# S5's V and W on one engine, attention's copies on another, K's rows on a queue of their own

## The chip, the cores and the metric

The kernel runs on one core of a Trainium2 chip. The metric is device time in microseconds for one launch. The engines' names in the profile are PE (TensorE, matmuls) and PEld (its weight loads), DVE (VectorE), ACT (ScalarE), POOL (GpSimd) and SP (SyncE); a "q" behind a name is the engine's instruction queue, which also issues transfers.

## The reference, cut to what matters

Two blocks of a diffusion transformer on 256 latent and 256 context tokens, width 1024, all in float32. Block 0 mixes tokens with grouped-query attention, block 1 with an S5 state space; each is followed by a hierarchical mixture of 32 experts.

```python
def gqa_axial_attention(u_lat, u_ctx, cos, sin, w_qkv, q_gain, k_gain, w_o, need_ctx):
    def project(u):
        q, k, v = split(u @ w_qkv)               # 8 heads of Q, 2 of K and V, 128 wide
        return rmsnorm(q, q_gain), rmsnorm(k, k_gain), v
    ...                                          # rope on the latent q and k only
    o = softmax(q k^T * hd ** -0.5) v            # context attends to context, latent to both
    y = o @ w_o

def s5_discretise(a_re, a_im, log_dt, b_re, b_im):   # 2 directions, 64 groups, 64 states, 16 channels
    dt = exp(log_dt)[:, None]
    ab = exp(a * dt)                             # complex
    bb = (ab - 1) / a * b
    ...
def s5_chunk_scan(u, ab, bb, c, s):
    x[t] = ab * x[t - 1] + bb @ u[t]
    y[t] = re(c @ x[t])

y = u * d_skip + scan(u) + flip(scan(flip(u)))   # then gelu, a linear unit with a gate, the residual
```

The S5 parameters do not depend on the tokens, so the operators that the scan needs are built while attention runs. The scan goes by blocks of 8 tokens: V holds B times the powers of the state's factor (tokens into state), W holds C times the powers (state into tokens), K is the kernel of one block (tokens into tokens), with the skip on its diagonal.

## The kernel before

**Attention** works on four tiles of 128 tokens, t = 0 and 1 the context, 2 and 3 the latent tokens. First each tile's K and V columns are projected (`project(t, 2)`), then twelve rounds of an outer loop follow, n = 0 to 11. In round n the loop runs side by side, one step of each at a time: `project(n % 4, n // 4)` for a half of Q (n < 8), `scores` for the half that was projected three rounds earlier, `values` for the one of four rounds earlier, and `steps(5, 2)`, which is five turns of two steps each of the background generator `par.work`. Between rounds stand a half of a modulation column (`mod.half`) and the transposes of Q (`turn_q`). Every engine executes its instructions in the order in which they were written, so this interleaving is the schedule.

`project` takes squares and a copy of the projection on ScalarE, their sum on VectorE (L359), the reciprocal root on GpSimd (`rstd`, L190, one power of 128 x 4 elements), then multiplies on VectorE: by the norm (L363), and by the gain (L365, context tiles) or by the rope tables (L371, L373, L374, latent tiles). `scores` has a matmul (L400), VectorE's maximum (L404), ScalarE's exponential (L405) and VectorE's reciprocal and scaling (L408, L409). `values` transposes the weights on TensorE, copies each transpose to SBUF (pT) and multiplies by V's half (L427). `evac` is a copy from PSUM, by turns on VectorE (L95) and ScalarE (L97).

**The background generator** `work` goes over 32 units of two S5 groups; four units share one set of operands (`operands`, L1245 to L1254, ten products on VectorE). A unit's `products` makes V in five VectorE operations (L1288, L1289, L1290, L1302, L1303) and W in five GpSimd operations of the same shape (L1297, L1298, L1299, L1304, L1305), each of 128 x 256 elements and with two inputs in SBUF. One unit later `turn` transposes V, copies it on ScalarE (vt, L1315) and sends it to DRAM by ScalarE's queue (L1317). Two units later `kernels` sends W by the same queue (L1323) and multiplies it on TensorE with `bd`, the block-diagonal operand (L1330). After four units `finish` copies the result on VectorE (ks, L1336, in a buffer of vt's), adds two pieces (L1340, L1341), sends four pieces of K's rows by ScalarE's queue (L1343, L1344), and copies the next operands into `bd` on VectorE (L1261, L1262). The generator has 145 steps; what the rounds leave over runs behind them (`bg.finish`).

Behind attention `tail` lends the SBUF of the stage to new buffers and SyncE's queue loads layer 1's modulation weights into them; the output projection (`out`, L443) follows, then the experts.

Of the kernel before, what the change touches and what calls it, by code (L numbers as in the profile page):

```python
# [9 lines left out]
F32 = mybir.dt.float32  # L10
# [4 lines left out]
AF = mybir.ActivationFunctionType  # L15
OP = mybir.AluOpType
# [227 lines left out]
def attention(c, mod, par, tail):  # L244
# [3 lines left out]
    with ExitStack() as ctx:  # L248
# [94 lines left out]
        def project(t, b):  # L343

            n = 2 if b == 2 else 4
            i = 1 if b == 2 else 0
            acc = bank("acc")
            for k in range(KT):
                if k and k % 2 == 0:
                    yield  # L350
                nc.tensor.matmul(acc, uT[:, k, 128 * t:128 * t + 128], wq[b][k // 4][:, k % 4, :],  # L351
                                 start=(k == 0), stop=(k == KT - 1))
            yield
            q = pk.tile([128, 4, HD], F32, name="qk", tag="qk", bufs=3)[:, 0:n]
            sq = pk.tile([128, 4, HD], F32, name="sq", tag="sq", bufs=2)[:, 0:n]
            nr = pk.tile([128, 4], F32, name="nr", tag="nr", bufs=2)[:, 0:n]
            nc.scalar.activation(sq.rearrange("p h d -> p (h d)"), acc[:, 0:128 * n], AF.Square)
            nc.scalar.activation(q.rearrange("p h d -> p (h d)"), acc[:, 0:128 * n], AF.Copy)
            nc.vector.tensor_reduce(nr, sq, axis=AX.X, op=OP.add)  # L359
            rstd(c, nr, nr, HD)  # L360
            if b == 2:
                nc.vector.tensor_copy(vv[:, t, :], acc[:, 256:512])
            nc.vector.tensor_mul(q, q, nr[:, :, None].to_broadcast([128, n, HD]))  # L363
            if t < 2:
                nc.vector.tensor_mul(q, q, gb[:, i:i + 1, :].to_broadcast([128, n, HD]))  # L365
            else:
                s5 = sq.rearrange("p h (a s f) -> p h a s f", a=2, s=2)
                q5 = q.rearrange("p h (a s f) -> p h a s f", a=2, s=2)
                sn = tab[:, t - 2, 1, i, :].rearrange("p (a s f) -> p a s f", a=2, s=2)
                for w in range(2):  # L370
                    nc.vector.tensor_mul(s5[:, :, :, w, :], q5[:, :, :, 1 - w, :],  # L371
                                         sn[:, None, :, w, :].to_broadcast([128, n, 2, 32]))
                nc.vector.tensor_mul(q, q, tab[:, t - 2, 0, i:i + 1, :].to_broadcast([128, n, HD]))  # L373
                nc.vector.tensor_add(q, q, sq)  # L374
            rot[t, b] = q
# [3 lines left out]
        def turn_k(t):  # L379
            p = bank("pt")  # L380
            for g in range(2):
                nc.tensor.transpose(p[:, 128 * g:128 * g + 128], rot[t, 2][:, g, :], c.ident)
            c.evac(kT[:, :, 128 * t:128 * t + 128], p[:, 0:256].rearrange("p (h d) -> p h d", h=2))

        def turn_q(t, g):
            x = lk.tile([128, 4, HD], F32, name="qT", tag="qT", bufs=3)
            p = bank("pt")
            for h in range(4):
                nc.tensor.transpose(p[:, 128 * h:128 * h + 128], rot[t, g][:, h, :], c.ident)
            c.evac(x, p.rearrange("p (h d) -> p h d", h=4))  # L390
            qT[t, g] = x

        P = {}
# [17 lines left out]
        def values(t, g):  # L411
            nk = 2 if t < 2 else 4
            yield
            pts = []
            for kt in range(nk + 1):
                if kt < nk:
                    p = bank("pt")
                    for h in range(4):
                        nc.tensor.transpose(p[:, 128 * h:128 * h + 128], P[t, g, h][:, 128 * kt:128 * kt + 128], c.ident)
                    x = lk.tile([128, 512], F32, name="pT", tag="pT", bufs=3)  # L420
                    c.evac(x, p)
                    pts.append(x)
                if kt == 1:
                    o = bank("acc")
                if kt:
                    k = kt - 1
                    nc.tensor.matmul(o, vv[:, k, 128 * g:128 * g + 128], pts[k], start=(k == 0), stop=(k == nk - 1))  # L427
                yield
            c.evac(oT[:, 4 * g:4 * g + 4, 128 * t:128 * t + 128], o.rearrange("p (h q) -> p h q", h=4))

        def rows():
            m2 = wk.tile([128, KT, 512], F32, name="m2", tag="uT").rearrange("p (j q) n -> p j (q n)", j=4)
# [20 lines left out]
                yield  # L453

        for t in range(4):
            together(project(t, 2), steps(5))
            if t:
                turn_k(t - 1)
        early.close()
# [3 lines left out]
            for h in range(2):  # L463
                fill[2 * ch + h - 3] = (ch, h)
        for n in range(12):
            s = [steps(5, 2)]
            if n < 8:
                s.append(project(n % 4, n // 4))
            if 0 <= n - 3 < 8:
                s.append(scores((n - 3) % 4, (n - 3) // 4))  # L470
            if 0 <= n - 4 < 8:
                s.append(values((n - 4) % 4, (n - 4) // 4))
            together(*s)
            if n == 0:
                turn_k(3)
            if n in fill:
                mod.half(0, *fill[n])
            if 0 <= n - 2 < 8:
                turn_q((n - 2) % 4, (n - 2) // 4)
            if n == 8:  # L480
                m2 = rows()
# [542 lines left out]
class S5Params:  # L1024
# [231 lines left out]

    def blocks(self, s):

        V = self.c.nc.vector
        for i in range(2):  # L1260
            V.tensor_copy(self.bd[i][0:64, :, 0:16], s[0:64, i])  # L1261
            V.tensor_copy(self.bd[i][64:128, :, 32:48], s[64:128, i])  # L1262

    def fetch(self, n):
        bc = self.wk.tile([128, 4, CH, 16], F32, name="bc", tag="bc", bufs=2)
# [3 lines left out]
    def work(self, bank, kbank):  # L1269
# [11 lines left out]
        def products(u, bc, s):  # L1281
            g, lg = slice(2 * u, 2 * u + 2), slice(2 * (u % per), 2 * (u % per) + 2)
            P = [x[:, g, ::-1][:, :, :, None].to_broadcast(sh) for x in self.P[1]]
            B = [s[:, i, lg][:, :, None, :].to_broadcast(sh) for i in (0, 2, 3)]
            vl = wk.tile([128, 2, 2, 128], F32, name="vl", tag="vl", bufs=2)
            v = [vl[:, i].rearrange("p g (i c) -> p g i c", i=8) for i in range(2)]
            v1 = wk.tile(sh, F32, name="v1", tag="v1")
            V.tensor_tensor(v1, B[0], P[2], op=OP.mult)  # L1288
            V.tensor_tensor(v[0], B[2], P[1], op=OP.mult)  # L1289
            V.tensor_tensor(v[1], B[1], P[0], op=OP.mult)  # L1290
            P = [x[:, g, :, None].to_broadcast(sh) for x in self.P[0]]
            C = [x[:, :, None, :].to_broadcast(sh) for x in (bc[:, 2, lg], s[:, 4, lg], s[:, 5, lg])]
            w = wk.tile([128, 2, 2, 128], F32, name="w", tag="w", bufs=5)
            wv = [w[:, :, i].rearrange("p g (i c) -> p g i c", i=8) for i in range(2)]
            w1 = wk.tile(sh, F32, name="w1", tag="w1")

            G.tensor_tensor(w1, C[0], P[2], op=OP.mult)  # L1297
            G.tensor_tensor(wv[0], C[2], P[1], op=OP.mult)  # L1298
            G.tensor_tensor(wv[1], C[1], P[0], op=OP.mult)  # L1299
            Q[u] = vl, w, s  # L1300
            yield
            V.tensor_tensor(v[0], v1, v[0], op=OP.subtract)  # L1302
            V.tensor_tensor(v[1], v1, v[1], op=OP.add)  # L1303
            G.tensor_tensor(wv[0], w1, wv[0], op=OP.subtract)  # L1304
            G.tensor_tensor(wv[1], wv[1], w1, op=OP.subtract)  # L1305
            yield

        def turn(u):
            vl, w, _ = Q[u]
            p = bank()  # L1310
            for i in range(2):
                for k in range(2):
                    nc.tensor.transpose(p[:, 256 * k + 128 * i:256 * k + 128 * i + 128], vl[:, i, k], c.ident)
            vt = wk.tile([128, 512], F32, name="vt", tag="vt", bufs=3)
            A.activation(vt, p, AF.Copy)  # L1315
            o = slice(512 * (u % per), 512 * (u % per) + 512)
            A.dma_start(self.vd[u // per][:, o], vt)  # L1317
# [13 lines left out]
                                     start=(i == 0), stop=(i == 1), skip_group_check=True)  # L1331

        def finish(n):
            ks = wk.tile([128, per, 128], F32, name="ks", tag="vt", bufs=3)
            kv = Q["kv"]
            V.tensor_copy(ks, kv)  # L1336
            gq = slice(per * n, per * n + per)
            for q in range(2):
                f, b = 64 * q, 64 * q + 32
                V.tensor_tensor(ks[f:f + 16, :, 0:16], kv[b:b + 16, :, 112:128], ks[f:f + 16, :, 0:16], op=OP.add)  # L1340
                V.tensor_add(ks[f:f + 16, :, 0:16], ks[f:f + 16, :, 0:16], self.dm[f:f + 16, gq])  # L1341
                dst = self.kd.rearrange("c (g q) n -> c q g n", q=2)[:, q, gq]
                A.dma_start(dst[:, :, 112:240], ks[f:f + 16])  # L1343
                A.dma_start(dst[:, :, 0:112], ks[b:b + 16, :, 0:112])  # L1344
            if n + 1 < NG // CH:
                self.blocks(Q[per * n + per][2])

# [509 lines left out]
```

## Time and profile before

| | |
|---|---|
| time, median of 3 runs | 1219.82 us (1219.55 to 1220.65) |
| profiled execution | 1219.71 us |
| its span, first to last instruction | 1217.9 us |
| busy in the span: PE, DVE, POOL, ACT | 1057.2, 802.1, 388.3, 270.0 us |
| mean granted TensorE clock | 0.948 of full speed |
| HBM traffic | 266 GB/s over the span |

A busy share is an average over stages with different limits; the change lies in the stage from about 45 to 314 us. A matmul that waits inside the pipeline counts as busy in places. An instruction's recorded time can overlap with the next one's on the same engine, so for a price both the recorded time and the distance from start to start are read.

### The profile page before, as it was taken

Reading aid. Unit: us, or ns where it says so; the run is one execution under the profiler, and the core shown is the slowest. Engines: PE = TensorE matmul, PEld = TensorE weight load, DVE = VectorE, ACT = ScalarE, POOL = GpSimd, SP = SyncE. Lnnn points to the kernel's source line nnn. Section 1 sums busy time; section 2 is a strip of 40 time slices with the busy share of each in tenths; the row PEclk is TensorE's granted clock in tenths of the full one; section 3 lists DMA queues with packets and bytes.
Section 4 is the critical chain, followed back from the end, with each engine's and each line's share of the span. In section 5 each row is a group of like instructions: output and inputs, shape, how many; then the busy total and the mean of one; then the engine's idle time right before and its main releaser. Section 6 shows DMA issues by size and latency. Waiting matters only on the chain. (4 is left out here: it accounts for less than half of the span.)

```text
span 1217.9 us, 18285 instructions
## 1 busy us (share of the span) xinstructions
PE 1057.2 (87%) x7011; PEld 619.4 (51%) x7011; DVE 802.1 (66%) x1679; ACT 270.0 (22%) x511; POOL 388.3 (32%) x473
## 2 busy tenths in 40 slices
PE   2888888857999799999999987787995999999997
PEld 0443444424444556666655543376674555555553
DVE  7788787888345526767778786588887344444444
ACT  3311223222112211111121211322433222112210
POOL 3566364554322202222355653346532000000000
PEclk9998899978999899999999999788997999999999
DMA  9845654652898488888676686669967799999951
GB/s 303 320 147 164 214 198 134 225 199 73 299 396 307 152 339 323 331 321 321 255 270 241 263 333 259 166 150 266 343 221 323 297 371 382 382 372 382 382 230 35
DMA packets 86892, 325.52 MB, mean 267 GB/s; under 512 B 9720, under 2 KB 19416, under 8 KB 68368
## 3 DMA queue, kind: packets, MB, share of 16 engines
q1 hardware_dynamic: 69296, 293.20, 65.9%
q10 hardware_dynamic: 13408, 20.01, 5.0%
q0 software_dynamic: 4096, 11.09, 2.8%
q8 instruction: 58, 0.95, 0.3%
q14 instruction: 34, 0.28, 0.1%
HBM read 305.37 MB, written 18.89 MB: 266 GB/s over the span
## 5 line engine op out<-in xcount | busy, mean ns | idle before, releaser
L801 PE MATMUL gu<-ring,xq 128*64 128x256 f32 x1136 | 162.1, 390 | 7.5 <-POOL pt L723 4.4
L870 POOL TENSOR_TENSOR h<-h,z 128x512 f32<-128x512 f32 x64 | 83.9, 1334 | 179.4 <-DVE z L857 179.4
L801 PE MATMUL gu<-more,xq 128*64 128x256 f32 x912 | 132.3, 387 | 1.7 <-DVE sl L806 1.7
L801 PEld LDWEIGHTS gu<-ring,xq 128*64 128x64 f32 x1136 | 91.6, 139 | 70.3 <-issue 30.8
L857 DVE TENSOR_TENSOR z<-co,gate 128x512 f32<-128x512 f32 x128 | 85.4, 685 | 40.7 <-PE co L866 31.3
L866 PE MATMUL co<-yh,oT 128*128 128x512 f32 x188 | 87.4, 465 | 16.8 <-DVE z L857 8.3
L801 PEld LDWEIGHTS gu<-more,xq 128*64 128x64 f32 x912 | 74.4, 138 | 50.6 <-issue 20.1
L351 PE MATMUL acc<-ring,uT 128*128 128x512 f32 x192 | 95.2, 629 | 4.7 <-ACT uT L327 3.4
L753 PEld LDWEIGHTS xt<-gq,parts 128*128 128x128 f32 x672 | 87.3, 191 | 10.5 <-issue 6.9
L753 PE MATMUL xt<-gq,parts 128*128 128x256 f32 x672 | 91.6, 286 | 0.0
L805 ACT ACTIVATE sl<-gu 64x256 f32<-64x256 f32 x64 | 24.1, 377 | 251.7 <-PE gu L801 251.7
L866 PE MATMUL co<-yl,oT 128*128 128x512 f32 x188 | 78.1, 415 | 0.6 <-DVE yl L851 0.6
L814 DVE COPY hT<-ht 128x128 f32<-128x128 f32 x64 | 18.4, 287 | 86.8 <-PE ht L812 86.6
L822 PE MATMUL y<-ring,hT 128*64 128x512 f32 x288 | 69.7, 604 | 0.4 <-DVE hT L814 0.4
L866 PEld LDWEIGHTS co<-yh,oT 128*128 128x128 f32 x188 | 35.8, 190 | 50.8 <-DVE z L857 19.9
L789 ACT ACTIVATE xq<-xt 128x512 f32<-128x512 f32 x56 | 33.4, 597 | 119.5 <-PE xt L753 119.5
L806 DVE TENSOR_TENSOR sl<-gu,sl 64x256 f32<-64x256 f32 x64 | 27.3, 426 | 47.0 <-ACT sl L805 45.7
L351 PEld LDWEIGHTS acc<-ring,uT 128*128 128x128 f32 x192 | 35.5, 200 | 40.2 <-issue 34.3
L822 PE MATMUL y<-more,hT 128*64 128x512 f32 x224 | 54.1, 604 | 0.4 <-DVE hT L814 0.4
L870 DVE TENSOR_TENSOR h<-h,z 128x512 f32<-128x512 f32 x64 | 50.5, 788 | 2.2
L141 PE MATMUL gv<-ring,cT 128*32 128x256 f32 x512 | 35.2, 420 | 18.3 <-DVE rs L189 16.3
L868 DVE TENSOR_TENSOR h<-h,co 128x512 f32<-128x512 f32 x64 | 41.1, 682 | 5.7 <-PE co L866 5.7
(424 smaller groups left out, 1954.8 us busy)
## 6 DMA issues: line engine op xcount, KB each, us to landing
ring<-moe_w_up SPq DMA_DIRECT2D x36, 1024.0 KB, 8.5
ring<-moe_w_down SPq DMA_DIRECT2D x36, 1024.0 KB, 9.4
ring<-moe_w_gate SPq DMA_DIRECT2D x35, 1024.0 KB, 6.8
ring<-mod_w SPq DMA_DIRECT2D x32, 1024.0 KB, 8.0
more<-moe_w_gate SPq DMA_DIRECT2D x29, 1024.0 KB, 7.0
more<-moe_w_up SPq DMA_DIRECT2D x28, 1024.0 KB, 9.2
more<-moe_w_down SPq DMA_DIRECT2D x28, 1024.0 KB, 11.2
more<-mod_w SPq DMA_DIRECT2D x16, 1024.0 KB, 8.7
```

The costliest lines, as they stand in the source:

```text
L141: nc.tensor.matmul(self.bank[i, b][32 * q:32 * q + 32, o:o + 256], self.cT[:, k, :], self.tiles[i, ch, k // 2][:, k % 2, 256 * q:256 * q + ...
L351: nc.tensor.matmul(acc, uT[:, k, 128 * t:128 * t + 128], wq[b][k // 4][:, k % 4, :], start=(k == 0), stop=(k == KT - 1))
L753: self.c.nc.tensor.matmul(p, x[:, k, :], g, start=(n + i == 0 and first), stop=(n + 1 == self.nt and i == 1), skip_group_check=True)
L789: nc.scalar.activation(out[-1][:, 2 * (s % 2):2 * (s % 2) + 2], p.rearrange("p (k n) -> p k n", k=2), AF.Copy)
L801: nc.tensor.matmul(p[s:s + 64, 0:HID], xT[k], w[k // 4][:, k % 4, :], start=(k == 0), stop=(k == KT - 1), skip_group_check=True)
L805: nc.scalar.activation(sl, p[0:64, 0:HID], AF.Silu)
L806: nc.vector.tensor_tensor(sl, p[64:128, 0:HID], sl, op=OP.mult)
L822: self.c.nc.tensor.matmul(p[o:o + 64, :], hT[:, f, :], wd[f][:, 512 * n:512 * n + 512], start=(f == 0), stop=(f == 1), skip_group_check=True)
L857: self.c.nc.vector.tensor_tensor(z, p, self.gate[j][:, 512 * f:512 * f + 512], op=OP.mult)
L866: nc.tensor.matmul(p, oh[:, 128 * n:128 * n + 128], y, start=(i == 0), stop=(i + 1 == len(rows)))
L868: nc.vector.tensor_tensor(h, h, p, op=OP.add)
L870: (nc.gpsimd if f else nc.vector).tensor_tensor(h, h, self.gated(p, j, f), op=OP.add)
```

## The change

V's and W's ten operations are all on VectorE, in four steps of the generator (V's three products, W's three, V's two sums, W's two) where there were two; the turns take two steps in the K and V part and three in the rounds. The copies of vv, kT, qT, pT and oT, which were VectorE's or alternated, are ScalarE's, and so are `bd`'s. On context tiles the two multiplications behind the norm become one fused operation for each head. K's rows have a buffer of their own (ks), vt has two in place of three, and the four transfers of a group are issued from GpSimd.

```diff
--- before.py
+++ after.py
@@ -359,11 +359,12 @@
             nc.vector.tensor_reduce(nr, sq, axis=AX.X, op=OP.add)
             rstd(c, nr, nr, HD)
             if b == 2:
-                nc.vector.tensor_copy(vv[:, t, :], acc[:, 256:512])
-            nc.vector.tensor_mul(q, q, nr[:, :, None].to_broadcast([128, n, HD]))
+                nc.scalar.activation(vv[:, t, :], acc[:, 256:512], AF.Copy)
             if t < 2:
-                nc.vector.tensor_mul(q, q, gb[:, i:i + 1, :].to_broadcast([128, n, HD]))
+                for h in range(n):
+                    nc.vector.scalar_tensor_tensor(q[:, h], q[:, h], nr[:, h:h + 1], gb[:, i, :], op0=OP.mult, op1=OP.mult)
             else:
+                nc.vector.tensor_mul(q, q, nr[:, :, None].to_broadcast([128, n, HD]))
                 s5 = sq.rearrange("p h (a s f) -> p h a s f", a=2, s=2)
                 q5 = q.rearrange("p h (a s f) -> p h a s f", a=2, s=2)
                 sn = tab[:, t - 2, 1, i, :].rearrange("p (a s f) -> p a s f", a=2, s=2)
@@ -380,14 +381,14 @@
             p = bank("pt")
             for g in range(2):
                 nc.tensor.transpose(p[:, 128 * g:128 * g + 128], rot[t, 2][:, g, :], c.ident)
-            c.evac(kT[:, :, 128 * t:128 * t + 128], p[:, 0:256].rearrange("p (h d) -> p h d", h=2))
+            nc.scalar.activation(kT[:, :, 128 * t:128 * t + 128], p[:, 0:256].rearrange("p (h d) -> p h d", h=2), AF.Copy)
 
         def turn_q(t, g):
             x = lk.tile([128, 4, HD], F32, name="qT", tag="qT", bufs=3)
             p = bank("pt")
             for h in range(4):
                 nc.tensor.transpose(p[:, 128 * h:128 * h + 128], rot[t, g][:, h, :], c.ident)
-            c.evac(x, p.rearrange("p (h d) -> p h d", h=4))
+            nc.scalar.activation(x, p.rearrange("p (h d) -> p h d", h=4), AF.Copy)
             qT[t, g] = x
 
         P = {}
@@ -418,7 +419,7 @@
                     for h in range(4):
                         nc.tensor.transpose(p[:, 128 * h:128 * h + 128], P[t, g, h][:, 128 * kt:128 * kt + 128], c.ident)
                     x = lk.tile([128, 512], F32, name="pT", tag="pT", bufs=3)
-                    c.evac(x, p)
+                    nc.scalar.activation(x, p, AF.Copy)
                     pts.append(x)
                 if kt == 1:
                     o = bank("acc")
@@ -426,7 +427,7 @@
                     k = kt - 1
                     nc.tensor.matmul(o, vv[:, k, 128 * g:128 * g + 128], pts[k], start=(k == 0), stop=(k == nk - 1))
                 yield
-            c.evac(oT[:, 4 * g:4 * g + 4, 128 * t:128 * t + 128], o.rearrange("p (h q) -> p h q", h=4))
+            nc.scalar.activation(oT[:, 4 * g:4 * g + 4, 128 * t:128 * t + 128], o.rearrange("p (h q) -> p h q", h=4), AF.Copy)
 
         def rows():
             m2 = wk.tile([128, KT, 512], F32, name="m2", tag="uT").rearrange("p (j q) n -> p j (q n)", j=4)
@@ -453,7 +454,7 @@
                 yield
 
         for t in range(4):
-            together(project(t, 2), steps(5))
+            together(project(t, 2), steps(5, 2))
             if t:
                 turn_k(t - 1)
         early.close()
@@ -463,7 +464,7 @@
             for h in range(2):
                 fill[2 * ch + h - 3] = (ch, h)
         for n in range(12):
-            s = [steps(5, 2)]
+            s = [steps(5, 3)]
             if n < 8:
                 s.append(project(n % 4, n // 4))
             if 0 <= n - 3 < 8:
@@ -1256,10 +1257,10 @@
 
     def blocks(self, s):
 
-        V = self.c.nc.vector
+        A = self.c.nc.scalar
         for i in range(2):
-            V.tensor_copy(self.bd[i][0:64, :, 0:16], s[0:64, i])
-            V.tensor_copy(self.bd[i][64:128, :, 32:48], s[64:128, i])
+            A.activation(self.bd[i][0:64, :, 0:16], s[0:64, i], AF.Copy)
+            A.activation(self.bd[i][64:128, :, 32:48], s[64:128, i], AF.Copy)
 
     def fetch(self, n):
         bc = self.wk.tile([128, 4, CH, 16], F32, name="bc", tag="bc", bufs=2)
@@ -1288,21 +1289,23 @@
             V.tensor_tensor(v1, B[0], P[2], op=OP.mult)
             V.tensor_tensor(v[0], B[2], P[1], op=OP.mult)
             V.tensor_tensor(v[1], B[1], P[0], op=OP.mult)
+            yield
             P = [x[:, g, :, None].to_broadcast(sh) for x in self.P[0]]
             C = [x[:, :, None, :].to_broadcast(sh) for x in (bc[:, 2, lg], s[:, 4, lg], s[:, 5, lg])]
             w = wk.tile([128, 2, 2, 128], F32, name="w", tag="w", bufs=5)
             wv = [w[:, :, i].rearrange("p g (i c) -> p g i c", i=8) for i in range(2)]
             w1 = wk.tile(sh, F32, name="w1", tag="w1")
 
-            G.tensor_tensor(w1, C[0], P[2], op=OP.mult)
-            G.tensor_tensor(wv[0], C[2], P[1], op=OP.mult)
-            G.tensor_tensor(wv[1], C[1], P[0], op=OP.mult)
+            V.tensor_tensor(w1, C[0], P[2], op=OP.mult)
+            V.tensor_tensor(wv[0], C[2], P[1], op=OP.mult)
+            V.tensor_tensor(wv[1], C[1], P[0], op=OP.mult)
             Q[u] = vl, w, s
             yield
             V.tensor_tensor(v[0], v1, v[0], op=OP.subtract)
             V.tensor_tensor(v[1], v1, v[1], op=OP.add)
-            G.tensor_tensor(wv[0], w1, wv[0], op=OP.subtract)
-            G.tensor_tensor(wv[1], wv[1], w1, op=OP.subtract)
+            yield
+            V.tensor_tensor(wv[0], w1, wv[0], op=OP.subtract)
+            V.tensor_tensor(wv[1], wv[1], w1, op=OP.subtract)
             yield
 
         def turn(u):
@@ -1311,7 +1314,7 @@
             for i in range(2):
                 for k in range(2):
                     nc.tensor.transpose(p[:, 256 * k + 128 * i:256 * k + 128 * i + 128], vl[:, i, k], c.ident)
-            vt = wk.tile([128, 512], F32, name="vt", tag="vt", bufs=3)
+            vt = wk.tile([128, 512], F32, name="vt", tag="vt", bufs=2)
             A.activation(vt, p, AF.Copy)
             o = slice(512 * (u % per), 512 * (u % per) + 512)
             A.dma_start(self.vd[u // per][:, o], vt)
@@ -1331,7 +1334,7 @@
                                      start=(i == 0), stop=(i == 1), skip_group_check=True)
 
         def finish(n):
-            ks = wk.tile([128, per, 128], F32, name="ks", tag="vt", bufs=3)
+            ks = wk.tile([128, per, 128], F32, name="ks", tag="ks")
             kv = Q["kv"]
             V.tensor_copy(ks, kv)
             gq = slice(per * n, per * n + per)
@@ -1340,8 +1343,8 @@
                 V.tensor_tensor(ks[f:f + 16, :, 0:16], kv[b:b + 16, :, 112:128], ks[f:f + 16, :, 0:16], op=OP.add)
                 V.tensor_add(ks[f:f + 16, :, 0:16], ks[f:f + 16, :, 0:16], self.dm[f:f + 16, gq])
                 dst = self.kd.rearrange("c (g q) n -> c q g n", q=2)[:, q, gq]
-                A.dma_start(dst[:, :, 112:240], ks[f:f + 16])
-                A.dma_start(dst[:, :, 0:112], ks[b:b + 16, :, 0:112])
+                nc.gpsimd.dma_start(dst[:, :, 112:240], ks[f:f + 16])
+                nc.gpsimd.dma_start(dst[:, :, 0:112], ks[b:b + 16, :, 0:112])
             if n + 1 < NG // CH:
                 self.blocks(Q[per * n + per][2])
```

## Rows read from the trace of the kernel before

**Rows 1.** Busy time by stretches: us, then PE, PEld, DVE, ACT, POOL (instructions), clock, DMA.

```profile
171.00:191.00 20.00, 19.28 (x112) 10.25 (x110) 14.91 (x37) 6.18 (x15) 10.55 (x16) 1.00 0.60 188
...
257.20:277.50 20.30, 11.13 (x51) 6.02 (x50) 16.32 (x31) 4.78 (x11) 11.40 (x18) 0.75 0.60 214
...
45.00:314.30 269.30, 217.20 (x1081) 111.28 (x1081) 222.85 (x499) 65.54 (x150) 143.14 (x193) 0.92 0.52 174
```

**Rows 2.** Waits, 66 to 306 us: total us, times, longest.

```profile
ACT pr L405 <- DVE mx L404: 107.6, 30, 10.1
...
ACT vt L1315 <- DMA s5k<-ks: 14.5, 2, 9.6
```

**Rows 3.** SyncE's queue, its waits from 225 to 420 us.

```profile
SPq L88 <- PE acc L427: 54.3, 1, 54.3
```

**Rows 4.** Timeline of VectorE, first V operation and what follows the fifth: start, us.

```profile
140.29 0.41 DVE L1288 TENSOR_TENSOR v<-ops,P 128x256 f32<-128x256 f32 x1
...
141.96 0.15 DVE L408 RECIPROCAL mx<-mx 128x1 f32<-128x1 f32 x1
```

**Rows 5.** Timeline from 103 us, GpSimd's W and VectorE's V side by side.

```profile
103.63 0.90 POOL L1305 TENSOR_TENSOR w<-w,w 128x256 f32<-128x256 f32 x1
103.87 0.94 DVE L1289 TENSOR_TENSOR vl<-ops,P 128x256 f32<-128x256 f32 x1
```

**Rows 6.** VectorE's groups, 45 to 314.3 us: busy us, mean ns, idle before.

```profile
L1289 DVE TENSOR_TENSOR vl<-ops,P 128x256 f32<-128x256 f32 x32 | 19.3, 604 | 0.0
...
L1302 DVE TENSOR_TENSOR vl<-v,vl 128x256 f32<-128x256 f32 x32 | 16.5, 516 | 0.0
...
L363 DVE TENSOR_TENSOR qk<-qk,nr 128x512 f32<-128x512 f32 x8 | 8.3, 1032 | 9.1 <-POOL nr L190 9.1
L95 DVE COPY pT<-pt 128x512 f32<-128x512 f32 x12 | 8.2, 682 | 3.7 <-PE pt L419 3.7
L1261 DVE COPY bd<-ops 64x128 f32<-64x128 f32 x16 | 7.1, 446 | 0.5
L1262 DVE COPY bd<-ops 64x128 f32<-64x128 f32 x16 | 6.9, 429 | 0.2
...
L371 DVE TENSOR_TENSOR sq<-qk,tab 128x256 f32<-128x256 f32 x8 | 6.2, 808 | 0.1
...
L95 DVE COPY oT<-acc 128x512 f32<-128x512 f32 x7 | 4.8, 683 | 2.5 <-PE acc L427 2.5
...
L1254 DVE TENSOR_TENSOR ops<-ops 128x128 f32<-128x128 f32 x7 | 4.1, 584 | 0.0
L365 DVE TENSOR_TENSOR qk<-qk,gb 128x512 f32<-128x512 f32 x4 | 3.9, 981 | 0.1
```

**Rows 7.** Single lines: ns least/median/most, first and last start; transfers' landing.

```profile
L1254 DVE TENSOR_TENSOR ops<-ops x8: 286/700/704, 39.6 to 281.4; 128x128 f32<-128x128 f32 x8
...
L1220 DVE SCALAR_TENSOR_TENSOR ph<-ph x8: 424/424/426, 602.1 to 723.6; 128x256 f32<-128x256 f32 x8
...
L1175 ACT ACTIVATE P<-pw x4: 1047/1066/1082, 26.0 to 28.9; 64x512 f32<-64x512 f32 x4
...
L190 POOL TENSOR_TENSOR nr<-rs,mhalf x12: 695/1008/1046, 53.7 to 235.7; 128x4 f32<-128x4 f32 x8, 128x2 f32<-128x2 f32 x4
...
L1266 POOL DMA_DIRECT2D bc<-s_bc x8: 756/830/867, 29.9 to 238.5; - x8
...
DMA to landing us min/median/max: 3.2/3.6/9.0
...
L1317 ACTq DMA_DIRECT2D s5v<-vt x32: 326/327/345, 53.2 to 309.7; - x32
...
DMA to landing us min/median/max: 2.4/2.6/7.7
```

**Rows 8.** Timeline of VectorE, L363 while GpSimd computes nothing.

```profile
98.24 0.69 DVE L363 TENSOR_TENSOR qk<-qk,nr 128x512 f32<-128x512 f32 x1 [1.12 <-POOL nr L190]
```

**Rows 9.** Timeline of TensorE, the out-projection's start; in brackets its idle time before.

```profile
314.29 7.11 PE L443 MATMUL oa<-ring,oT 128*128 128x512 f32 x16 [1.74 <-DVE ks L1341]
```

## The prediction

> **What bounds the kernel now.** I read the busy time by stretches first. From 45 to 314.3 us (attention, with S5's operator work threaded through it) VectorE is busy 222.85 of 269.3 us, TensorE 217.20, GpSimd 143.14, ScalarE 65.54 [rows 1]. No engine is full: they hand work to each other in program order, and VectorE is nearest to being the bound. The exception is a projection-heavy part such as 171 to 191, where TensorE has 19.28 of 20 us and VectorE 14.91; late in the stage (257 to 277) it is the reverse, 16.32 on VectorE against 11.13 [rows 1].
>
> Next, who waits: ScalarE's exponentials stood 107.6 us behind VectorE's row maxima, up to 10.1 at a time [rows 2]. So what is late is VectorE.
>
> Then, who waits for the stage: SyncE's queue stood 54.3 us, in one wait, on attention's last matmul, because the buffers for layer 1's weights lie where attention's tiles were [rows 3]. A stage that ends earlier starts those loads earlier, so I pass its gain on to the end at full value.
>
> Last, why VectorE is late. Alone, the five V operations of a unit start at 140.29, and the next instruction starts at 141.96: 0.335 us a step, though each is recorded at 0.42 [rows 4]. Beside GpSimd's W the same operation takes 0.94 us, and starts where a W operation of 0.90 ends its hold [rows 5]. Over all 32 units the five lines average 516 to 604 ns [rows 6]. Other two-input steps show the same pair of prices: one line takes 286 ns at the least and 700 at the median [rows 7]. The two engines hold each other up.
>
> **The change, part by part** (VectorE's time over the whole stage).
>
> *V and W.* V's five lines are recorded at 89.0 us in all (19.3 for the first, 16.5 for the last [rows 6]). Consecutive steps overlap by 0.08 (0.42 against 0.335 [rows 4]), so 160 of them take 89.0 - 12.8 = 76.2. After it there are 320 steps. W on VectorE does not occur in the trace. It is bounded by V, whose shape and pattern it shares: 0.335 below, 0.94 above. With W gone from GpSimd, nothing there reads SBUF for long (the rstd power is 12 operations, 1008 ns at the median [rows 7]), so I take the lower: 320 x 0.335 = 107.2, or +31.0.
>
> By a rule this sum would turn: the Trainium skill ("VectorE: DVE Perf Modes", section "The DRAIN you can't avoid") says that the next operation does not start until the pipeline has emptied, with a section of its own for those that start earlier. By the rule each step would cost its recorded 0.42, and the sum +58. The trace disagrees where V runs alone: 0.335 from start to start.
>
> *bd's copies* go to ScalarE: two lines, 7.1 and 6.9 us [rows 6], -14.0. Their price on ScalarE is not shown. Its nearest row is the copy of 64 x 512 elements at 1.066 us [rows 7], four times as many, so between near 0 and 1.07 each; I take 0.3, 32 times, 10 us. ScalarE has 204 us free; if that cover were gone, the four copies of a group (1.2 us) would stand ahead of the next kernel matmuls, where VectorE's now stand.
>
> *Attention's copies* leave VectorE: 12 of pT, 7 of oT at 0.68 [rows 6], 0.60 net of the overlap, -11.4. Four of V's halves, two of kT and one of qT, six of them half as wide, add an estimated 2.6. Together -14.0. On ScalarE they queue behind the exponentials, but those are what VectorE held up.
>
> *The fused gains* (context tiles). Two steps of 1032 and 981 ns [rows 6] become four of 128 elements. A fused step with a column operand is not shown. Below it lies a 128 x 128 product, 286 ns recorded [rows 7], 0.20 net; above it a fused step of 128 x 256, 424 [rows 7], 0.34 net. That one costs what a plain product of the same size does, so I take 0.20. Per Q tile 1.85 becomes 0.8, four times: -4.2; two K tiles at half width: -1. Together -5.2.
>
> *The steps that stay* lose GpSimd's company. L363, on the four latent Q tiles, goes from 1.03 to the 0.69 that it takes alone [rows 6, 8]: 4 x 0.34 = 1.4. L371 goes from 0.81 to V's 0.42, its shape: 8 x 0.39 = 3.1. L1254 goes from 0.58 to 0.29 [rows 6, 7]: 7 x 0.30 = 2.1. L373 and L374 have L363's shape and count, L1253 has L1254's, and I take the same for them: 2.7 and 2.1. Together -11.4; narrower forms are left out.
>
> *VectorE's sum:* 31.0 - 14.0 - 14.0 - 5.2 - 11.4 = **-13.6**, to 209.3 us. Its idle 46.4 us are hand-overs, repeated every round, so I let them shrink with the work: 13.6 x 269.3 / 222.85 = **-16.4**.
>
> *K's rows* leave ScalarE's queue. Now the queue stops at each of their issues until VectorE has made the rows, with the exponentials and vt behind it; and vt, which shares its buffers, waited 14.5 us in two waits for those rows to land [rows 2]. What reaches the path lies between 0 and 14.5. A vt copy that stands holds a bank of PSUM which TensorE's next transposes need, but ScalarE is idle most of the time; I take half, **-7**. On GpSimd an issue costs 0.83 us [rows 7], four a group 3.3. Queued behind them is only rstd's power, for which VectorE's L363 waits. Counting the generator's steps, a group's end falls into the round of a power once, at n = 4; VectorE has some 2 us to do between the two, so about +1, at most 3.3. vt with two buffers is reused two units later, some 17 us (269.3 / 32 x 2); its transfer lands in 2.6 us at the median and 7.7 at most [rows 7], so this is hidden. The rows' own buffer is reused a group later, longer still.
>
> Here too a rule speaks against the edit: the Trainium skill ("SBUF — State Buffer", section "SBUF: two separate sides") says that while VectorE runs in a mode with two ports, GpSimd cannot write its transfers' descriptors. The trace has GpSimd's own loads in this stage landing in 3.6 us at the median, 9.0 at most [rows 7]; were every K transfer that late, no unit would wait for it.
>
> *Pacing.* Four short steps a unit make 209 steps in place of 145 (my count). With 2 and 3 a round, 222 are offered, where 142 were before. So three steps, the last group's end among them, no longer follow attention: now TensorE stands idle for 1.74 us before the out-projection, for that end [rows 9], and about **-2** comes back. Three steps a round are at most 3 x 3 x 0.335 = 3 us ahead of a row maximum, no more than one contended V now.
>
> **Sum:** -16.4 - 7 + 1 - 2 = **-24.4 us**. The profiled execution took 1219.71 us, 1217.9 of them span; it stands 0.1 below the median of three, 1219.82. That gives 1195.3, on the median's scale 1195.4; I say 1195.
>
> **The rivals.**
> *TensorE takes over.* It is at 96% from 171 to 191 [rows 1], and the change gives it no less to do. If the projection-heavy part, 147 to 239 us, shortens by nothing, 16.4 x 92 / 269.3 = 5.6 are lost; if hand-overs do not shrink outside it either, (16.4 - 13.6) x 177 / 269.3 = 1.8, and if K's rows give nothing, 7. That leaves 24.4 - 14.4 = 10: 1209 to 1210. For it speaks that row; against it, that VectorE's contended steps [rows 5] lie in these stretches too. Chance 0.15.
> *A step costs more on VectorE than V alone does.* The place is the 320 steps. All I take off is 76.2 + 14.0 + 14.0 + 5.2 + 11.4 = 120.8, so from 0.38 us a step (120.8 / 320) VectorE gains no more; the whole kernel turns at about 0.40, where 128.0 - 120.8 = 7.2, x 1.21, eats the 8 that K's rows and the pacing give. At the recorded 0.42: 134.4 - 120.8 = +13.6, x 1.21 = +16.5, less 8: 1228. Against it stand the undisturbed rows [rows 4]; for it, that short steps are broken up by steps of other kinds. With the rule on the emptied pipeline above it is the same case. Chance 0.08.
> *GpSimd's queue delays the powers* at all of the eight group ends, 3.3 us each, 26 in all: 1195 + 25 = 1220, on the line. Against it: my count finds one. Chance 0.02.
> *The stage shortens and the end does not move* (layer 1's loads bind): 1219 to 1221. Against it the one wait of 54.3 us. Chance 0.05.
> *More than forecast:* if half of VectorE's 46.4 us idle was GpSimd's hold at one remove and goes with it, 23 in place of the 2.8 above: 1175. Chance 0.08.
>
> **How the numbers follow.** The forecast (15 to 34 us off, 1186 to 1205) has 0.62. Faster 0.62 + 0.15 + 0.08 = 0.85; within 0.2% (2.4 us, about what this kernel's spread of 1.1 us lets one tell) 0.05; slower 0.10. The range leaves out the slower cases, the unmoved end and about half of "more than forecast": 1182 to 1212.
>
> **What would show it.** After the change V's and W's ten lines should each average near 0.42 recorded, GpSimd should be near idle, L363, L371 and L1254 near their free prices, VectorE at about 209 us in a stage of about 245, ScalarE near 90, and the last matmul of attention some 20 us earlier with every later stage moved by as much. V or W above 0.5, TensorE near full over the whole stage, or layer 1's first loads early with experts that start as before, would each prove a step wrong.

## The result, and the profile after

The changed kernel takes 1184.95 us (median of 4 runs, 1181.48 to 1188.51) against 1219.68; the ratio is 0.9715, interval 0.9683 to 0.9748. It is 34.7 us faster; 24.4 were forecast, and the range of 1182 to 1212 holds the median near its lower end. The profiled execution took 1186.46 us, 33.3 less than the one that the forecast was made against.

The same stretch as in [rows 1], from 45 us to the out-projection's first matmul, which now comes at 283.1:

```profile
45.00:283.10 238.10, 210.92 (x1080) 107.99 (x1079) 198.33 (x606) 85.67 (x206) 39.90 (x63) 0.95 0.59 198
```

The stage lasts 238.1 us in place of 269.3, 31.2 less. VectorE lost 24.5 us of work though it has 107 more instructions; GpSimd went from 143.14 to 39.90; TensorE is now busy 89% of the stage, more than VectorE with 83%.

VectorE's groups in the stage, for [rows 6] (line numbers from 360 to 375 have moved by one to four, those behind L1289 by one to three):

```profile
L1290 DVE TENSOR_TENSOR vl<-ops,P 128x256 f32<-128x256 f32 x32 | 13.4, 419 | 0.6 <-PE pt L1316 0.6
...
L1307 DVE TENSOR_TENSOR w<-w,w 128x256 f32<-128x256 f32 x32 | 13.4, 417 | 0.0
...
L372 DVE TENSOR_TENSOR sq<-qk,tab 128x256 f32<-128x256 f32 x8 | 3.0, 422 | 0.1
...
L1255 DVE TENSOR_TENSOR ops<-ops 128x128 f32<-128x128 f32 x7 | 2.0, 285 | 0.0
```

All ten lines of V and W stand between 417 and 419 ns, where V's five had averages up to 604; L372 (L371 before) is at 422 for 808, L1255 (L1254) at 285 for 584, and by the same view L367 (L363) is at 692 for 1032. The price from start to start is the forecast's too, where the steps follow each other. VectorE's timeline, a unit's last steps on one engine:

```profile
97.32 0.42 DVE L1304 TENSOR_TENSOR vl<-v,vl 128x256 f32<-128x256 f32 x1
97.66 0.42 DVE L1305 TENSOR_TENSOR vl<-v,vl 128x256 f32<-128x256 f32 x1
97.99 0.42 DVE L1307 TENSOR_TENSOR w<-w,w 128x256 f32<-128x256 f32 x1
```

The waits in the stage, for [rows 2]:

```profile
ACT pr L406 <- DVE mx L405: 75.9, 31, 7.6
```

The exponentials stand 75.9 us behind the maxima, for 107.6. vt no longer waits for K's rows. Behind the stage everything is shifted as a block. The 50 us from 300 in the kernel after, and the 50 us from 331 in the kernel before, by the same view as [rows 1]:

```profile
300.00:350.00 50.00, 49.42 (x383) 23.19 (x382) 24.66 (x87) 9.77 (x22) 11.00 (x11) 1.00 0.98 369
```

```profile
331.00:381.00 50.00, 49.43 (x383) 23.31 (x382) 24.61 (x88) 9.77 (x22) 11.02 (x11) 1.00 0.97 369
```

The same 383 matmuls, the same busy times, the same 369 GB/s: 31 us are passed on. The experts' first matmul comes at 397.7 for 428.7. The last 2 us of the 33.3 come later, and no run here was made for them.

### The profile page after: what moved, and what is told of

It is laid out like the page before. It is cut to its first block, busy times and chain, and to the rows that moved or that the text cites. A ratio compares the mean times of both kernels' runs of the same rounds, so it can differ in the third digit from the quotient of the medians.

```text
span 1184.7 us, 18273 instructions
## 1 busy us (share of the span) xinstructions
PE 1046.8 (88%) x7011; PEld 613.2 (52%) x7011; DVE 777.1 (66%) x1789; ACT 291.3 (25%) x569; POOL 284.8 (24%) x345
## 5 line engine op out<-in xcount | busy, mean ns | idle before, releaser
L802 PE MATMUL gu<-ring,xq 128*64 128x256 f32 x1136 | 165.1, 396 | 8.0 <-POOL pt L724 4.4
L351 PE MATMUL acc<-ring,uT 128*128 128x512 f32 x192 | 95.3, 630 | 2.9 <-ACT uT L327 2.9
L754 PEld LDWEIGHTS xt<-gq,parts 128*128 128x128 f32 x672 | 85.8, 188 | 10.6 <-issue 7.2
```

The source lines that it names most:

```text
L754: self.c.nc.tensor.matmul(p, x[:, k, :], g, start=(n + i == 0 and first), stop=(n + 1 == self.nt and i == 1), skip_group_check=True)
L802: nc.tensor.matmul(p[s:s + 64, 0:HID], xT[k], w[k // 4][:, k % 4, :], start=(k == 0), stop=(k == KT - 1), skip_group_check=True)
```

## The experiments

Two theories. **A**, the forecast's: VectorE sets the stage, the time follows the sum of its work, and its idle time shrinks in proportion. **B**: what cost the time was GpSimd's W beside VectorE, in held steps and in the waits that follow from them. They differ on the parts alone. By A the copies bring nearly everything and W on VectorE costs time; by B it is the other way.

**Each part alone, put into the kernel before.** W's five lines:

```diff
-            G.tensor_tensor(w1, C[0], P[2], op=OP.mult)
+            V.tensor_tensor(w1, C[0], P[2], op=OP.mult)
...
```

> The kernel before with W's five operations on VectorE and nothing else. Theory A (the gain follows VectorE's sum of work): 160 more steps at 0.335 us, V, bd's copies and the other steps at their free prices; some +31 - 11 - 7 = +13 us of work, so 1225 to 1240. Rival B (the gain is the end of the hold between the two engines, idle time included): as fast as before or faster, 1195 to 1220.

Measured: 1205.86 us, ratio 0.9909 (0.9881 to 0.9937): 12.7 us faster. Its stage, up to the out-projection at 302.2:

```profile
45.00:302.20 257.20, 214.01 (x1081) 109.61 (x1081) 222.46 (x660) 66.20 (x151) 25.69 (x36) 0.94 0.55 183
```

161 more instructions on VectorE by this row, and its busy time is 222.46 where it was 222.85. Its groups show how:

```profile
L1303 DVE TENSOR_TENSOR vl<-v,vl 128x256 f32<-128x256 f32 x32 | 13.4, 418 | 0.0
...
L363 DVE TENSOR_TENSOR qk<-qk,nr 128x512 f32<-128x512 f32 x8 | 5.5, 693 | 9.5 <-POOL nr L190 8.4 <-ACT vt L1315 1.2
...
L1262 DVE COPY bd<-ops 64x128 f32<-64x128 f32 x16 | 3.6, 224 | 0.2
```

V at 418, L363 at 693 for 1032, bd's copies at 3.6 us a line (L1261 like L1262) for 7.1 and 6.9 [rows 6]. What W adds, the others give back, and of the 12.1 us by which the stage is shorter 11.7 are idle time of VectorE. A is missed by 19 us or more.

The copies of attention and of bd (`c.evac`, `V.tensor_copy` to `nc.scalar.activation(..., AF.Copy)`), alone:

> The kernel before with attention's copies and bd's copies on ScalarE and nothing else. Theory A: 28 us of work off VectorE, so some 25 to 34 us faster, 1186 to 1195. Rival B: GpSimd's W still holds V up, so at most 15 us faster, 1205 to 1217.

1213.04 us, ratio 0.9962 (0.9941 to 0.9983): 5.5 us faster. Stage to 309.0:

```profile
45.00:309.00 264.00, 217.75 (x1080) 111.29 (x1081) 203.72 (x442) 87.67 (x209) 144.61 (x193) 0.92 0.53 178
```

19.1 us of work left VectorE where 28 were forecast: V's five lines, still beside GpSimd's W, take 95.3 us in all for 89.0. The stage lost 5.3 us, and VectorE's idle time rose from 46.4 to 60.3. Two waits of this run:

```profile
DVE ks L1336 <- PE kp L1330: 11.9, 1, 11.9
ACT bd L1261 <- DMA s5k<-ks: 11.8, 3, 9.3
```

The first, 2.3 us in the kernel before, is at the end of the stage and makes up much of the rise. VectorE's last product ends at 295.6 us, and until the last group's result is there, at 307.5, it has nothing left to do; TensorE, which has attention's last matmuls to do in that time, is busy for 10.8 of these 11.9 us. VectorE's work had stopped setting the end. The second is bd's: its copies are now on ScalarE, behind the issue of K's rows, which waits in the same queue. TensorE waits 3.8 us for them in the whole stage.

K's rows on GpSimd, with their own buffer, alone:

```diff
-            vt = wk.tile([128, 512], F32, name="vt", tag="vt", bufs=3)
+            vt = wk.tile([128, 512], F32, name="vt", tag="vt", bufs=2)
...
-            ks = wk.tile([128, per, 128], F32, name="ks", tag="vt", bufs=3)
+            ks = wk.tile([128, per, 128], F32, name="ks", tag="ks")
...
-                A.dma_start(dst[:, :, 112:240], ks[f:f + 16])
+                nc.gpsimd.dma_start(dst[:, :, 112:240], ks[f:f + 16])
...
```

> The kernel before with K's rows on GpSimd's queue and in a buffer of their own. Predicted as 7 us off and 1 on: 1213. If it is hidden: 1219 to 1221. If GpSimd's queue, now with W in it, stops at the issues until VectorE has made the rows: slower, 1222 or more.

1224.97 us, ratio 1.0058 (1.0039 to 1.0076): 6.4 us slower. Its stage, up to 322.9, and what GpSimd waited for:

```profile
45.00:322.90 277.90, 225.78 (x1080) 113.81 (x1080) 233.75 (x499) 65.42 (x150) 156.65 (x217) 0.89 0.50 169
...
POOL s5k L1343 <- DVE ks L1340: 47.3, 7, 12.1
```

GpSimd's queue stood 47.3 us at the issues until VectorE had made the rows, with W behind it. The loss does not come as waiting for W: TensorE waited 6.6 us for it, 7.7 in the kernel before. It comes as longer steps: V's five lines took 108.9 us in all for 89.0, and VectorE's busy time rose by 10.9 us. That the standing queue brings W beside V more often is inferred from this. In the full change the queue stands longer, 75.4 us by the same view, but W has left it: the powers and a few transfers are behind, and VectorE waits 13.1 us for the powers where it waited 11.1.

W and the copies together:

> The kernel before with W on VectorE and the copies on ScalarE, without the fused gains, the four short steps and K's rows. Theory A: VectorE -14.0 - 14.0 + 13 + 7 (bd's relief counted once) = -8 to -14, so 1203 to 1210. Rival B: most of the whole change's 35 us, 1185 to 1195.

1197.15 us, ratio 0.9825 (0.9806 to 0.9843): 21.4 us faster, between the two forecasts and more than the 12.7 + 5.5 of the parts. TensorE still waits for bd here, 9.6 us.

**Each part taken out of the changed kernel.** W back on GpSimd:

> The changed kernel with W's five operations on GpSimd again, in the same steps. Theory A (VectorE's sum of work): 54 us of steps leave VectorE, contention comes back with some 45 us; 1180 to 1195, within 10 us of the changed kernel. Rival B (the hold is what cost the time): most of the gain is lost, 1205 to 1220.

1212.21 us, ratio to the kernel before 0.995 (0.9933 to 0.9966): 27 of the 35 us are lost. Stage to 305.0:

```profile
45.00:305.00 260.00, 216.96 (x1080) 111.03 (x1081) 211.69 (x450) 86.85 (x208) 154.95 (x221) 0.93 0.53 182
```

156 instructions fewer on VectorE than after, and 13.4 us more work; its idle time is 8.5 us more as well. The 27 us are not the hold alone, because W stands here behind the issues of K's rows, at which GpSimd's queue waits 50.3 us in all. The copies back:

> The changed kernel with all the copies where they were: 28 us of work come back to VectorE, which is busy 198 of 238 us in the stage. Theory A: 1205 to 1220. Rival B: 1190 to 1200.

1194.77 us, ratio 0.9806 (0.979 to 0.9823): 10 us are lost, as B said. Stage to 292.1:

```profile
45.00:292.10 247.10, 211.69 (x1080) 107.91 (x1079) 219.04 (x664) 63.80 (x147) 40.03 (x63) 0.95 0.58 192
```

20.7 us of work came back to VectorE, and the stage grew by 9.0: the rest went into idle time, which fell from 39.8 to 28.1 us. K's rows back:

> The changed kernel with K's rows issued by ScalarE from a buffer shared with vt. Predicted for this part: 6 us net, so 1191. If hidden: 1185. If ScalarE's queue, now with more in it, stands for the rows: above 1195.

1195.61 us, ratio 0.9805 (0.9763 to 0.9848), runs from 1190.57 to 1201.63: some 11 us are lost, with a wide interval. vt waits for K's rows nowhere in this run, though it shares a buffer with them again. TensorE's wait for bd in this run, and what is left of it after the change:

```profile
PE kp L1333 <- ACT bd L1263: 11.0, 7, 3.9
```

```profile
PE kp L1333 <- ACT bd L1263: 0.8, 2, 0.6
```

The short steps back (no yield inside the two halves, `steps(5)` and `steps(5, 2)`):

> The changed kernel with two steps a unit and one or two a turn, as before, so that the same work comes in longer steps and its end runs behind attention. Predicted for this part: 2 us (1187). If the short steps are what lets the maxima through: 1195 or more.

1191.48 us, ratio 0.9774 (0.9758 to 0.9791): 6.5 us are lost, between the two cases named. The out-projection starts at 285.9, 2.8 later than after the change; with the spread of the changed kernel's own runs (7 us) the rest is not settled.

**Is it the hold, or the waiting for W?** The changed kernel with GpSimd work that nobody reads, once reading SBUF, once only writing:

```diff
+            dum = wk.tile([128, 512], F32, name="dum", tag="dum")
+            dv = dum[:, 0:256].rearrange("p (g i c) -> p g i c", g=2, i=8)
+            for _ in range(5):
+                G.tensor_tensor(dv, C[0], P[2], op=OP.mult)     # gp_writes: G.memset(dum, 0.0)
```

> The changed kernel with five GpSimd products of W's shape a unit whose result nobody reads (W's buffers are four in place of five to make room). Nothing waits for them but the rstd powers behind them in GpSimd's queue. If two engines that both read SBUF hold each other: V's and W's lines on VectorE go from 0.42 to 0.55 or more and the kernel to 1205 or more. If W on GpSimd cost time only because TensorE and ScalarE's queue waited for it: 0.42 stays and the time is 1182 to 1192.

> The control: the same place, the same buffers and five GpSimd instructions of about the same length a unit, but memsets, which read nothing. If reading is what holds: VectorE's lines stay at 0.42 and the time at 1182 to 1192. If any GpSimd work (its port, its queue ahead of the powers) costs the time: as slow as the run with products.

With products 1246.11 us, ratio 1.021 (1.0171 to 1.025): 61 us slower than the changed kernel. With memsets 1192.36, ratio 0.9775 (0.9739 to 0.9811). The stage and one line of each, first with products:

```profile
45.00:340.10 295.10, 233.07 (x1081) 116.73 (x1082) 258.65 (x609) 86.54 (x207) 150.86 (x219) 0.87 0.47 160
...
L1304 DVE TENSOR_TENSOR w<-ops,P 128x256 f32<-128x256 f32 x32 | 18.4, 574 | 0.0
...
L1301 POOL TENSOR_TENSOR dum<-bc,P 128x256 f32<-128x256 f32 x156 | 111.1, 712 | 10.9
```

and with memsets:

```profile
45.00:283.00 238.00, 206.12 (x1078) 105.85 (x1077) 202.95 (x608) 85.27 (x205) 124.02 (x221) 0.97 0.59 199
...
L1304 DVE TENSOR_TENSOR w<-ops,P 128x256 f32<-128x256 f32 x32 | 13.4, 418 | 0.0
...
L1301 POOL MEMSET dum<- 128x512 f32 x158 | 84.7, 536 | 7.9
```

GpSimd is busy 151 us and 124, and VectorE waits alike for the powers behind that work (14.3 and 15.8 us in all). Only with products do V and W go to 489 to 574 ns, VectorE to 258.65 us and the stage to 295.1; with memsets it ends where it did, at 283.0. So the hold, with next to nobody waiting for GpSimd's result, costs some 57 us of stage here: VectorE's busy time is 55.7 us more, its idle time 1.4. TensorE, with the same matmuls, is busy for 233.07 us with products and 206.12 with memsets, at a mean granted clock of 0.87 and 0.97; what this adds, the two runs do not separate. The cost is shown for products that read; the 7 us by which the memset run's median lies above the changed kernel's do not stand in its profiled stage and stay open.

W on GpSimd, with its transfers on GpSimd's queue as well:

```diff
-            A.dma_start(self.wd[n][:, o], w.rearrange("p g i n -> p (g i n)"))
+            G.dma_start(self.wd[n][:, o], w.rearrange("p g i n -> p (g i n)"))
```

> W on GpSimd again (1212 with its transfers on ScalarE's queue), with W's transfers on GpSimd's own queue, so that ScalarE no longer stands for W. If that standing is a large part of the loss: 1200 or less. If the hold is: 1208 to 1220.

1221.64 us, ratio 1.0022 (1.0002 to 1.0043), slower than with them on ScalarE's queue by 9.4 and just above the case named for the hold. VectorE's busy time in the stage rose with it, from 211.69 to 226.78 us, with V's lines at 590 to 771 ns. So the run moved the hold too and does not price ScalarE's standing for W; it shows that these issues are dearer on GpSimd.

**A further step.** One yield between the power and the multiplications that wait for it:

```diff
             rstd(c, nr, nr, HD)
             if b == 2:
                 nc.scalar.activation(vv[:, t, :], acc[:, 256:512], AF.Copy)
+            yield
```

> The changed kernel with one yield between the rstd power and the multiplications that wait for it, so that VectorE has scores' last scaling to do meanwhile. It idles 13.1 us there now in twelve waits. If VectorE still sets the stage: 3 to 10 us faster, 1175 to 1182. If TensorE does by now (211 of 238 us busy): within 3 us of the changed kernel.

1183.39 us (6 runs), ratio 0.9693 (0.9664 to 0.9722). Its profiled stage ends at 277.3, 5.8 us before that of the changed kernel, but the medians differ by 1.6 us and the intervals overlap: not told apart.

## Why the prediction was right, and where it was not

*Where the gain goes.* Right. The stage shortened, and what lies behind it moved as a block by 31 us. The rival that the end would not move is out.

*What bounds.* Right in part. VectorE's contended steps were late: the exponentials' wait for the maxima fell from 107.6 to 75.9 us. But VectorE's work alone does not set the stage: 19.1 us off it gave 5.3, 20.7 us put back cost 9.0.

*The price of a step.* Right: 0.33 to 0.34 us from start to start, 0.42 recorded. The rival with 0.38 or more is out, and with it the rule of the emptied pipeline as a price of the sum. One reading was loose: in [rows 5] V's operation does not start where W's ends. W's runs from 103.63 to 104.53 us and V's starts at 103.87, so both are long side by side.

*VectorE's sum.* Mis-sized: 24.5 us came off, 13.6 were forecast. The term is "the steps that stay". The six lines that I had priced give 10.6 us (L363 4 x 0.34, L371 8 x 0.386, L1254 7 x 0.30, L1253 7 x 0.215, L373 and L374 together 2.5), for 11.4; those that I left out give some 9 more: L409 15.6 to 13.5 us, L329 from 776 to 406 ns a step (seven steps, three of which now lie ahead of 45 us), and the narrow forms of L363, L371, L373, L374 and L1341. The other terms held: bd's copies take 0.310 us on ScalarE for 0.3, an issue of K's rows 0.512 on GpSimd for 0.83, a fused head 0.347 recorded where I had taken 0.28.

*"Its idle 46.4 us ... shrink with the work".* In the full change 39.8 are left where the whole forecast leaves 35.6 (244.9 - 209.3), so the number was near. As a mechanism this step failed. The copies alone took 19.1 us of work away, and idle time rose by 13.8, much of it at the end of the stage; the copies put back added 20.7 us of work, and idle time fell by 11.7; W alone took next to no work away, and idle time fell by 11.7 as well (46.4 to 34.7). By A the singles came out wrong on both sides; theory A falls.

*Luck.* That the total lies in the range is in part luck. By the forecast's terms W alone adds 13 us of work and the copies take 28; W alone took 0.4, the copies 19.1, two errors of opposite sign. With the measured 24.5 us in place of 13.6 the forecast's own rule would give 24.5 x 269.3 / 222.85 = 29.6, and 37.6 with its 8 for K's rows and the pacing, against 34.7 measured: what made the forecast too small is VectorE's sum.

*What stands in its place.* GpSimd's products held VectorE's steps: W off GpSimd is worth 12.7 us alone and 27 in the changed kernel, where K's rows in GpSimd's queue are a part of it, and work that merely reads on GpSimd costs 61. The rival "more than forecast", which let the hold's idle time go with it, pointed the right way with too large a number. The Trainium skill ("SBUF — State Buffer", section "Who interferes with whom") says that a VectorE instruction with two inputs in SBUF contends with a GpSimd instruction that reads SBUF, and not with one that only writes; the two runs with unread work agree, 489 to 574 ns against 418.

*K's rows.* Forecast -7 + 1, measured -11 with a wide interval when taken out last, and +6.4 when put in first. I had valued the shared buffer; what counted was the queue, for with the buffer shared again vt waits for no rows. On ScalarE the issues stand ahead of bd's copies, which the same change puts there (11.0 us of TensorE's waiting, 0.8 without); on GpSimd they stand ahead of W, unless W has left, and V's steps grow (89.0 to 108.9 us). So the parts hang together: alone they change the time by -12.7, -5.5 and +6.4 us, a sum of -11.8, and all of them, with the fused gains and the short steps, by -34.7. The fused gains were not tried alone. The warning about GpSimd's transfers did not come true at a cost that shows: K's rows land in 3.4 us at the median, 7.4 at most.

*Pacing.* -2 was forecast for the end of the stage; 2.8 us of the stage and 6.5 in all came with it, and what lies beyond the 2.8 is open.

*TensorE as the next bound.* Its 1209 to 1210 did not come, but it is at 89% of the stage now. That the change gives it no less to do was not so in time: with the same matmuls its busy time in the stage fell from 217.20 to 210.92 us, while its mean granted clock rose from 0.92 to 0.95. No run separates this part of the gain.

## What to carry to other kernels

Before work is moved between GpSimd and VectorE, read each step's least time beside its mean: where the mean lies well above the least, as with V's lines here (516 to 604 ns, 418 when free), moving the reading work to VectorE can cost it nothing, as here 160 steps did. A sum over one engine's work sizes a change only while the waits stay where they are; test the parts alone, because two that look independent may share a queue. In these runs a queue that issues a transfer stood until the data were made (47.3 and 75.4 us in all), so put such issues where nothing urgent is behind them.

## What the runs showed of the hardware beyond expectation

VectorE's single-input steps are held too: a scaling of 128 x 256 with column operands (L329) took 776 ns beside GpSimd's products and 406 without, and a copy of 64 x 128 (L1262) up to 1.9 us in the kernel before, and at most 226 ns with W on VectorE. The power of 128 x 4 elements on GpSimd takes 1.0 us even with GpSimd otherwise idle, and VectorE waits up to 1.2 us for each.
